# A hybrid decoder step: x turned by VectorE in 32x32 blocks instead of TensorE transposes, with w_in read in the matching row order

## The chip, the cores and the metric

The kernel runs on one core of one Trainium2 chip. The metric is the device time of one execution in microseconds; a kernel's time is the median of its runs. A profile is one execution of its own, recorded by the hardware profiler. In it PE is TensorE's matmul, PEld its weight load, DVE is VectorE, ACT is ScalarE, POOL is GpSimd, and SP is the engine that issues most DMAs.

## The reference

One layer of a hybrid decoder over 256 prompt tokens and 8 x 4 sample tokens, 288 in all, with D = 2048. Cut to what matters here:

```python
def _rmsnorm(x, g):                       # x: (tokens, 2048)
    y = x * lax.rsqrt(jnp.mean(x * x, axis=-1, keepdims=True) + EPS)
    return y * g

xn = _rmsnorm(x, norm_mix)
u = xn @ w_in                             # w_in: (2048, 15408), cut into ten pieces: z, xBC, dt, q, k, v, r, g, gates
...                                       # SSD branch, GLA branch, merged by gates, projected by w_mix_out
h = x + merged                            # the residual
...                                       # cross-attention into 256 memory tokens, then a ConvFFN

mn = _rmsnorm(mem_prompt, norm_mem)       # 256 memory tokens
p_mem_k, p_mem_v = mn @ w_ck, mn @ w_cv   # (256, 2048) each, outputs
```

Everything is float32.

## The kernel before

**Matmuls.** A float32 product is made of three: every operand is split into a high part rounded to fp32r and the low rest, and hi x hi, hi x lo and lo x hi are summed in PSUM. For weights `wsplit` does this: ACT casts `raw` into `whi` (line 103) and DVE subtracts to give `wlo` (line 105). `raw` has three buffers (`RB = 3`) and `whi` and `wlo` five each (`WB = 5`). The loads of `raw` are issued by SP in one queue: a load waits until the buffer three loads back has been split, and what stands behind it in the queue waits too.

**Layout.** The activations stand transposed: channels on the partitions, tokens along the free axis, in 16 k-tiles of 128 channels. `X(k)` gives the high and low part of k-tile k of the normalized x. In the kernel before, channel 128k + p is on partition p of k-tile k, and `proj` reads its weights in the same order ("(k p) n -> p k n").

**The first stages.** `mem_proj` makes one 512-column piece of the memory keys or values: 16 k-tiles of six 128x512 matmuls (lines 315, 316, 319), their weights loaded two k-tiles (512 KB) at a time. The first one, of `w_ck`, is written out by hand and takes the memory rows `mt` in with it, by TensorE transposes. Then `weave` runs two of them beside `x_norm` (the stage of x_norm, 32 k-tiles), and two more beside `x_prep` (the stage of x_prep, 32 k-tiles). `weave(main, bg, n_main, n_bg)` advances the background generator in proportion to the main one.

- `x_norm` loads x in nine pieces (`x_load`, on SP): the 32 sample rows into `xs` and quarters of the 256 prompt rows into `xp`, tokens on the partitions. ACT squares and sums them (line 391) in twelve pieces into `sp4`; `ss` becomes 1/rms for each token. It also makes the per-channel vectors: `vrow` is turned on TensorE and copied to `vcol`. At its end `dg`, a diagonal matrix of `ss`, goes through a matmul with ones (line 431), so that `rtok` holds 1/rms of each token on every partition (a DVE copy, line 432).
- `x_prep` turns x: for each k-tile three 128x128 TensorE transposes into PSUM (line 442), an ACT copy into `xf` (line 445), stored to the DRAM tile `x_d` two k-tiles at a time by SP (line 447), a product with `rtok` on DVE (`xr`, line 449), and the split with the gain `norm_mix` into `X` (lines 184 and 185). Last it turns `srow`, the carried rows of the SSD convolution.

After that come the projection of dt and g (`dt_load`, lines 487 to 495: the first reader of X), more `mem_proj`, and the SSD and GLA branches, whose projections all read `w_in` by `proj`. The residual is read back from `x_d` by `load_x` (line 1334, DMAs of POOL into `hx`) when `w_mix_out` is projected, and added at line 1352.

**What sets the order.** The tile framework orders the instructions of each engine by a simulated timeline (`schedule_with_timeline_sim=True`); the first `mem_proj` is excepted, and a DMA marked `keep_in_program_order` keeps its place. The order inside an engine is then fixed, and engines wait for each other by semaphores.

Of the kernel before, what the change touches and what calls it, by code (L numbers as in the profile page):

```python
# [16 lines left out]
P = 128  # L17
# [25 lines left out]
def hybrid_step(ctx: ExitStack, tc: tile.TileContext, I: dict, O: list):  # L43
# [44 lines left out]
    names = [("norm_mem", 16), ("norm_mix", 16), ("ssd_norm", 16), ("norm_cross", 16), ("norm_ffn", 16),  # L88
# [6 lines left out]
    def vec(name):  # L95
        o, n = vofs[name]
        return vcol[:, o:o + n]
# [59 lines left out]

    def proj(w, c0, ncol, X, nk, cons, row0=0):
        def load(k0, kn):
            return wload(w[row0 + k0 * P:row0 + (k0 + kn) * P, c0:c0 + ncol].rearrange("(k p) n -> p k n", p=P))  # L160
        return proj_w(load, ncol, X, nk, cons)
# [100 lines left out]
    x_d = dram.tile([P, KT, T], F32, name="x_d")  # L262
# [3 lines left out]
    with pool("p0") as p0:  # L266
# [7 lines left out]
        mt = p0.tile([P, 2, D], F32, tag="rows", name="mt")  # L274
# [81 lines left out]
        xp = p0.tile([P, 2, D], F32, tag="rows", name="xp")  # L356
        xs = p0.tile([P, D], F32, name="xs")
        G.memset(xs, 0.0)
        xts = [xp[:, 0, :], xp[:, 1, :], xs]
# [16 lines left out]
        def x_load(n):  # L376

            if n == 0:
                d = nc.sync.dma_start(out=xs[0:NS], in_=I["x_sample"].rearrange("b l d -> (b l) d"))
            else:  # L380
                i, cs = (n - 1) // 4, slice((n - 1) % 4 * 512, (n - 1) % 4 * 512 + 512)
                d = nc.sync.dma_start(out=xp[:, i, cs], in_=I["x_prompt"][0, i * P:(i + 1) * P, cs])
            tc.keep_in_program_order(d)

        def x_norm():
            sp4 = p0.tile([P, 3, 4], F32, name="sp4")
            ss = p0.tile([P, 3], F32, name="ss")

            def square(i, q):
                junk = p0.tile([P, 512], F32, name="junk")  # L390
                S.activation(junk, xts[i][:, q * 512:(q + 1) * 512], ACT.Square, accum_out=sp4[:, i, q:q + 1])

            for step in range(23):
                if step % 2 and step < 18:
                    x_load(step // 2)
                if step == 3:

                    V.tensor_reduce(mrs, mss, AX.X, ALU.add)
                    S.activation(mrs, mrs, ACT.Ln, scale=1.0 / D, bias=epsc[:, 0:1])
                    S.activation(mrs, mrs, ACT.Exp, scale=-0.5)  # L400
                if step == 6:
                    held.pop()()
                if step > 6 and step % 2 == 0 and step < 15:
                    square(2, step // 2 - 4)
                if step > 6 and step % 2:
                    square((step - 7) // 8, (step - 7) // 2 % 4)
                yield
            V.tensor_reduce(ss, sp4, AX.X, ALU.add)
            S.activation(ss, ss, ACT.Ln, scale=1.0 / D, bias=epsc[:, 0:1])
            S.activation(ss, ss, ACT.Exp, scale=-0.5)  # L410
# [15 lines left out]
            dg = p0.tile([P, 3, P], F32, name="dg")  # L426
            for i in range(3):
                V.tensor_scalar(dg[:, i, :], ident, ss[:, i:i + 1], None, ALU.mult)
            yield
            a = mm_tile()  # L430
            MM(a[:, 0:T], ones, dg.rearrange("p c t -> p (c t)")[:, 0:T], start=True, stop=True)
            V.tensor_copy(rtok, a[:, 0:T])
# [3 lines left out]
        def x_prep():  # L436

            gx = vec("norm_mix")
            for k in range(KT):
                a = mm_tile()  # L440
                for i, xt in enumerate(xts):
                    TR(a[:, i * P:(i + 1) * P], xt[:, k * P:(k + 1) * P], ident)
                if k % 2 == 0:
                    xf = p0.tile([P, 2, T], F32, tag="xf", bufs=3, name="xf")
                S.copy(xf[:, k % 2, :], a[:, 0:T])
                if k % 2:
                    nc.sync.dma_start(out=x_d[:, k - 1:k + 1, :], in_=xf)
                xr = p0.tile([P, T], F32, tag="xr", bufs=3, name="xr")
                V.tensor_tensor(xr, a[:, 0:T], rtok, ALU.mult)
                split_from(*X(k), xr, gx[:, k:k + 1])  # L450
                yield
            for q in range(2):
                a = mm_tile()
                for i in range(3):
                    TR(a[:, i * 96:(i + 1) * 96], srow[:, 3 * q + i, :], ident[0:96, 0:96])
                V.tensor_copy(scst[:, q * 12:(q + 1) * 12, 0:3 * NB], a[:, 0:288].rearrange("p (t c) -> p t c", c=3 * NB))
                yield
# [16 lines left out]
        weave(chain(mem_proj(I["w_cv"], 0, o_pmv), mem_proj(I["w_ck"], 1, o_pmk)), x_norm(), 2 * KT, 28)  # L474
# [11 lines left out]
        def dt_load(k0, kn):  # L486
            raw = wp.tile([P, kn, 112], F32, tag="raw", bufs=RB, name="raw")
            for o, c0, n in ((0, O_DT, 32), (32, O_G, 16)):
                nc.sync.dma_start(out=raw[:, :, o:o + n],
                                  in_=I["w_in"][k0 * P:(k0 + kn) * P, c0:c0 + n].rearrange("(k p) n -> p k n", p=P))  # L490
# [841 lines left out]
    def load_x(j2):  # L1332
        m = pc.tile([P, 2, T], F32, tag="hx", bufs=3, name="hx")
        G.dma_start(out=m, in_=x_d[:, 2 * j2:2 * j2 + 2, :])
# [496 lines left out]
```

## Time and profile before

| | |
|---|---|
| median of 3 runs | 2519.35 us (2517.22 to 2526.04) |
| profiled execution | 2522.44 us |
| its span, first to last instruction | 2520.7 us |
| PE busy | 2502.4 us (99%) |
| DVE, ACT, POOL busy | 1753.1, 1346.9, 392.8 us |
| DMA | 521.95 MB, mean 207 GB/s |
| stage of x_norm | about 33 to 76.5 us |
| stage of x_prep | 76.5 to 127.15 us |

The profiled execution is a run of its own, 3.1 us over the median. Busy is the time in which an engine had at least one instruction under way; matmuls overlap, so a matmul's duration is longer than the distance to the next one. A row of a group gives line, engine, operation, output<-inputs, shapes and count, then busy us and mean ns, then the engine's idle time before them and what ended it.

### The profile page before, as it was taken

How to read it: one execution, taken by the hardware profiler on the slowest of the kernel's cores; microseconds unless marked ns; L12 is line 12 of the kernel's file. 1: busy time of each engine (PE TensorE's matmuls, PEld its weight loads, DVE VectorE, ACT ScalarE, POOL GpSimd, SP SyncE). 2: the span in 40 equal slices, each digit the busy share in tenths (PEclk: the TensorE clock that was granted, in tenths of full speed). 3: DMA queues.
4: the chain of work that ended last, by engine and by line, in shares of the span. 5: the costliest groups of instructions: out<-in, count | busy, mean ns of one | idle time of the engine just before them, and what ended most of it. 6: DMA issues, size and time to landing. Idle time of an engine off the chain costs nothing.

```text
span 2520.7 us, 50431 instructions
## 1 busy us (share of the span) xinstructions
PE 2502.4 (99%) x18914; PEld 2411.9 (96%) x18914; DVE 1753.1 (70%) x3752; ACT 1346.9 (53%) x2736; POOL 392.8 (16%) x729
## 2 busy tenths in 40 slices
PE   9999999999999999999999999999999999999998
PEld 8889999998999999999999989999999999999998
DVE  6656777796867666666666677567777677676765
ACT  7655647655463655454445544555555455454545
POOL 3002133342300010000001122402111001020010
PEclk9999999999999999999999999999999999999999
DMA  8776587767868675867778599655555555555553
GB/s 268 221 218 196 171 251 210 228 196 210 245 188 275 183 251 175 248 207 263 202 224 267 180 327 323 213 159 178 170 171 173 170 168 171 170 175 169 168 171 129
DMA packets 442021, 521.95 MB, mean 207 GB/s; under 512 B 26876, under 2 KB 390236, under 8 KB 441712
## 3 DMA queue, kind: packets, MB, share of 16 engines
q1 hardware_dynamic: 407728, 422.34, 54.3%
q0 software_dynamic: 34016, 96.38, 12.0%
q8 instruction: 148, 2.42, 0.4%
q14 instruction: 97, 0.79, 0.1%
q10 hardware_dynamic: 32, 0.01, 0.0%
HBM read 473.13 MB, written 45.48 MB: 206 GB/s over the span
## 4 chain that ended last, share of the span: by engine, by line
PE 95%; DMA 2%; DVE 1%; ACT 1%; issue 0%; POOL 0%; DVEq 0%; ACTq 0%; POOLq 0%
PE acc L148 27%; PE acc L147 27%; PE acc L151 26%; PE acc L315 2%; PE acc L316 2%; PE acc L319 2%; PE la L1541 1%; PE mm L1159 1%; PE la L1150 1%; DMA sqr<-in_state_ssd_dram 1%; PE la L1483 1%; PE mm L1123 1%; DMA sin<-in_state_ssd_dram 1%; DMA raw<-in_w_gla_out_dram 0%; POOL sqr L731 0%
## 5 line engine op out<-in xcount | busy, mean ns | idle before, releaser
L103 ACT CAST whi<-raw 128x512 fp32r<-128x512 f32 x1464 | 897.3, 618 | 1011.9 <-PE acc L148 783.6
L105 DVE TENSOR_TENSOR wlo<-raw,whi 128x512 fp32r<-128x512 f32 x1464 | 997.2, 687 | 607.9 <-ACT whi L103 590.5
L147 PE MATMUL acc<-xn,whi 128*128 128x288 f32 (+1 forms) x1936 | 550.2, 299 | 0.0
L148 PE MATMUL acc<-xn,whi 128*128 128x288 f32 (+1 forms) x1936 | 542.0, 296 | 0.0
L151 PE MATMUL acc<-xn,wlo 128*128 128x288 f32 (+1 forms) x1936 | 414.3, 295 | 0.0
L148 PE MATMUL acc<-hf,whi 128*128 128x288 f32 x1408 | 393.2, 295 | 0.0
L147 PE MATMUL acc<-hf,whi 128*128 128x288 f32 x1408 | 389.0, 292 | 0.0
L147 PEld LDWEIGHTS acc<-xn,whi 128*128 128x128 f32 (+1 forms) x1936 | 364.4, 188 | 9.9 <-issue 7.5
L148 PEld LDWEIGHTS acc<-xn,whi 128*128 128x128 f32 (+1 forms) x1936 | 364.5, 188 | 6.6 <-issue 4.6
L151 PEld LDWEIGHTS acc<-xn,wlo 128*128 128x128 f32 (+1 forms) x1936 | 310.5, 188 | 1.6 <-issue 1.3
L151 PE MATMUL acc<-hf,wlo 128*128 128x288 f32 x1408 | 294.5, 290 | 0.0
L148 PEld LDWEIGHTS acc<-hf,whi 128*128 128x128 f32 x1408 | 264.5, 188 | 0.1
L147 PEld LDWEIGHTS acc<-hf,whi 128*128 128x128 f32 x1408 | 264.0, 188 | 0.1
L151 PEld LDWEIGHTS acc<-hf,wlo 128*128 128x128 f32 x1408 | 226.3, 188 | 0.0
L148 PE MATMUL acc<-pr,whi 128*128 128x288 f32 x704 | 196.6, 295 | 0.0
L147 PE MATMUL acc<-pr,whi 128*128 128x288 f32 x704 | 195.0, 293 | 0.0
L151 PE MATMUL acc<-pr,wlo 128*128 128x288 f32 x704 | 147.4, 290 | 0.0
L147 PE MATMUL acc<-un,whi 128*128 128x288 f32 x512 | 145.3, 300 | 1.2 <-DVE mb L961 0.8
L148 PE MATMUL acc<-un,whi 128*128 128x288 f32 x512 | 143.0, 295 | 0.0
L1655 POOL COPY fsp<-fst 128x16 f32<-128x16 f32 x88 | 37.1, 424 | 656.5 <-DVE av L1667 422.0
L148 PEld LDWEIGHTS acc<-pr,whi 128*128 128x128 f32 x704 | 132.3, 188 | 0.0
L147 PEld LDWEIGHTS acc<-pr,whi 128*128 128x128 f32 x704 | 132.0, 188 | 0.0
(516 smaller groups left out, 4283.4 us busy)
## 6 DMA issues: line engine op xcount, KB each, us to landing
raw<-in_w_in_dram SPq DMA_DIRECT2D x240, 512.0 KB
raw<-in_w_up_dram SPq DMA_DIRECT2D x176, 512.0 KB
raw<-in_w_down_dram SPq DMA_DIRECT2D x88, 512.0 KB
raw<-in_w_cv_dram SPq DMA_DIRECT2D x32, 512.0 KB
raw<-in_w_ssd_out_dram SPq DMA_DIRECT2D x32, 512.0 KB
sin<-in_state_gla_dram POOLq DMA_DIRECT2D x32, 512.0 KB, 5.6
out_dram<-sin SPq DMA_DIRECT2D x32, 512.0 KB
raw<-in_w_gla_out_dram SPq DMA_DIRECT2D x32, 512.0 KB
```

What stands on the lines that cost most here:

```text
L103: S.copy(hi, raw)
L105: V.tensor_tensor(lo, raw, hi, ALU.subtract)
L147: MM(a, hi[:, k, cs], xh, start=(k0 + s0 + k == 0), stop=False)
L148: MM(a, hi[:, k, cs], xl, start=False, stop=False)
L151: MM(a, lo[:, k, cs], xh, start=False, stop=(k0 + s0 + k == nk - 1))
L315: MM(accs[m], mn_hi[:, kk, ms_], hi[:, 0, :], start=(kk == 0), stop=False)
L316: MM(accs[m], mn_lo[:, kk, ms_], hi[:, 0, :], start=False, stop=False)
L319: MM(accs[m], mn_hi[:, kk, ms_], lo[:, 0, :], start=False, stop=(kk == KT - 1))
L1123: MM(a, kt[:, i, k * P:(k + 1) * P], vt[i], start=True, stop=True)
L1150: MM(osa[NS * j:NS * j + NS, :], qdm[:, k, b, :], sins[b][:, k, :], start=False, stop=(q == 1 and k == 0))
L1159: MM(a, kb[:, k * P:(k + 1) * P], vst, start=True, stop=True)
L1655: G.tensor_copy(sp[:, :, 0:2], st.rearrange("p (b k) -> p b k", k=2))
```

## The change

x is loaded as nine blocks of 32 tokens into `xrow`: the 2048 channels of a token are cut into four quarters, which lie on the partitions 32i + t. One DVE transpose of 32x32 blocks for each block, reading every 16th element, gives `xT`, in which channel 16p + k stands on partition p of k-tile k. The gain comes in that order by a DMA (`gmix`), and `w_in` is read in that order by `rows_of`, so that the sum over channels is the same. The squares are taken of the same nine blocks; `fold4` times their sums goes through the matmul with ones, which sums the four quarters, and ACT makes 1/rms of the result by Ln and Exp over 128x288. The 48 TensorE transposes and the `xf` copies are gone; `x_d` is now (2048, 288) in channel order, stored from `xT` in program order and read back by k-tiles of 128 channels. The tile of `mt` grows to nine pieces and shares its place with `xrow`.

In the built program the order on every engine is the same from the projection of dt and g on. Before it, the first DVE transpose stands behind the third-next `wlo` after the memory's sum of squares, the others behind every second or third `wlo`; two of the x loads stand one weight load earlier on SP; and the stores of `x_d` begin behind the first weight load of the stage of x_prep.

```diff
@@ -85,7 +85,7 @@
 
     vcol = const.tile([P, 116], F32, name="vcol")
     scw = const.tile([P, 96], F32, name="scw")
-    names = [("norm_mem", 16), ("norm_mix", 16), ("ssd_norm", 16), ("norm_cross", 16), ("norm_ffn", 16),
+    names = [("norm_mem", 16), ("ssd_norm", 16), ("norm_cross", 16), ("norm_ffn", 16),
              ("b_gla_gate", 8), ("gla_norm", 4), ("ssd_conv_b", 24)]
     vofs = {}
     dcol = const.tile([P, KT], F32, name="dcol")
@@ -155,9 +155,15 @@
                     flush()
                 yield
 
+    def rows_of(w, row0, k0, kn, c0, ncol):
+
+        if w is I["w_in"]:
+            return w.rearrange("(p k) n -> p k n", k=KT)[:, k0:k0 + kn, c0:c0 + ncol]
+        return w[row0 + k0 * P:row0 + (k0 + kn) * P, c0:c0 + ncol].rearrange("(k p) n -> p k n", p=P)
+
     def proj(w, c0, ncol, X, nk, cons, row0=0):
         def load(k0, kn):
-            return wload(w[row0 + k0 * P:row0 + (k0 + kn) * P, c0:c0 + ncol].rearrange("(k p) n -> p k n", p=P))
+            return wload(rows_of(w, row0, k0, kn, c0, ncol))
         return proj_w(load, ncol, X, nk, cons)
 
     def run(*gens):
@@ -259,7 +265,7 @@
     ma_d = dram.tile([P, KT, T], F32, name="ma_d")
     mg_d = dram.tile([P, KT, T], F32, name="mg_d")
     ga_d = dram.tile([P, KT // 2, T], F32, name="ga_d")
-    x_d = dram.tile([P, KT, T], F32, name="x_d")
+    x_d = dram.tile([D, T], F32, name="x_d")
     h_d = dram.tile([P, KT, T], F32, name="h_d")
 
     X = halves(bigr, "xn")
@@ -271,7 +277,7 @@
         S.dma_start(out=mrow, in_=I["norm_mem"].rearrange("(t p) -> t p", p=P))
         S.preload_act_table_set(LNEXP)
         S.copy(epsc[:, 2:3], epsc[:, 0:1])
-        mt = p0.tile([P, 2, D], F32, tag="rows", name="mt")
+        mt = p0.tile([P, 9, 512], F32, tag="rows", name="mt")[:, 0:8].rearrange("p (i q) d -> p i (q d)", i=2)
 
         def mem_load(k0):
             cs = slice(k0 * P, (k0 + 2) * P)
@@ -353,10 +359,10 @@
             run(mem_proj(I["w_ck"], 0, o_pmk, prep_mem, held))
 
 
-        xp = p0.tile([P, 2, D], F32, tag="rows", name="xp")
-        xs = p0.tile([P, D], F32, name="xs")
-        G.memset(xs, 0.0)
-        xts = [xp[:, 0, :], xp[:, 1, :], xs]
+        xrow = p0.tile([P, 9, 512], F32, tag="rows", name="xrow")
+        xT = p0.tile([P, KT, T], F32, name="xT")
+        gmix = p0.tile([P, KT], F32, name="gmix")
+        G.dma_start(out=gmix, in_=I["norm_mix"].rearrange("(p k) -> p k", k=KT))
         G.dma_start(out=dtb, in_=I["ssd_dt_bias"].unsqueeze(1))
         G.dma_start(out=alog, in_=I["ssd_A_log"].unsqueeze(1))
         r = 0
@@ -375,22 +381,19 @@
 
         def x_load(n):
 
-            if n == 0:
-                d = nc.sync.dma_start(out=xs[0:NS], in_=I["x_sample"].rearrange("b l d -> (b l) d"))
-            else:
-                i, cs = (n - 1) // 4, slice((n - 1) % 4 * 512, (n - 1) % 4 * 512 + 512)
-                d = nc.sync.dma_start(out=xp[:, i, cs], in_=I["x_prompt"][0, i * P:(i + 1) * P, cs])
-            tc.keep_in_program_order(d)
+            b = n - 1 if n else 8
+            src = I["x_prompt"][0, 32 * b:32 * b + 32] if n else I["x_sample"].rearrange("b l d -> (b l) d")
+            tc.keep_in_program_order(nc.sync.dma_start(out=xrow[:, b, :], in_=src.rearrange("t (i d) -> i t d", i=4)))
 
         def x_norm():
-            sp4 = p0.tile([P, 3, 4], F32, name="sp4")
-            ss = p0.tile([P, 3], F32, name="ss")
-
-            def square(i, q):
+            ss = p0.tile([P, 9], F32, name="ss")
+
+            def square(b):
                 junk = p0.tile([P, 512], F32, name="junk")
-                S.activation(junk, xts[i][:, q * 512:(q + 1) * 512], ACT.Square, accum_out=sp4[:, i, q:q + 1])
-
-            for step in range(23):
+                S.activation(junk, xrow[:, b, :], ACT.Square, accum_out=ss[:, b:b + 1])
+                V.transpose(xT[:, :, 32 * b:32 * b + 32], xrow[:, b, :].rearrange("p (x j) -> p j x", j=KT))
+
+            for step in range(27):
                 if step % 2 and step < 18:
                     x_load(step // 2)
                 if step == 3:
@@ -400,14 +403,11 @@
                     S.activation(mrs, mrs, ACT.Exp, scale=-0.5)
                 if step == 6:
                     held.pop()()
-                if step > 6 and step % 2 == 0 and step < 15:
-                    square(2, step // 2 - 4)
-                if step > 6 and step % 2:
-                    square((step - 7) // 8, (step - 7) // 2 % 4)
+                if step == 9:
+                    square(8)
+                if step > 10 and step % 2:
+                    square((step - 11) // 2)
                 yield
-            V.tensor_reduce(ss, sp4, AX.X, ALU.add)
-            S.activation(ss, ss, ACT.Ln, scale=1.0 / D, bias=epsc[:, 0:1])
-            S.activation(ss, ss, ACT.Exp, scale=-0.5)
             yield
             a = mm_tile()
             TR(a[:, 0:r], vrow[0:r, :], ident[0:r, 0:r])
@@ -423,31 +423,25 @@
                               drow[64 * e:64 * e + 64, :].rearrange("p (t e) -> p e t", e=2)[:, e, :])
             yield
 
-            dg = p0.tile([P, 3, P], F32, name="dg")
-            for i in range(3):
-                V.tensor_scalar(dg[:, i, :], ident, ss[:, i:i + 1], None, ALU.mult)
+            dg = p0.tile([P, 9, NS], F32, name="dg")
+            V.tensor_tensor(dg, fold4.unsqueeze(1).to_broadcast([P, 9, NS]), ss.unsqueeze(2).to_broadcast([P, 9, NS]), ALU.mult)
             yield
             a = mm_tile()
-            MM(a[:, 0:T], ones, dg.rearrange("p c t -> p (c t)")[:, 0:T], start=True, stop=True)
-            V.tensor_copy(rtok, a[:, 0:T])
+            MM(a[:, 0:T], ones, dg.rearrange("p c t -> p (c t)"), start=True, stop=True)
+            S.activation(rtok, a[:, 0:T], ACT.Ln, scale=1.0 / D, bias=epsc[:, 0:1])
+            S.activation(rtok, rtok, ACT.Exp, scale=-0.5)
 
         rtok = p0.tile([P, T], F32, name="rtok")
 
         def x_prep():
 
-            gx = vec("norm_mix")
             for k in range(KT):
-                a = mm_tile()
-                for i, xt in enumerate(xts):
-                    TR(a[:, i * P:(i + 1) * P], xt[:, k * P:(k + 1) * P], ident)
                 if k % 2 == 0:
-                    xf = p0.tile([P, 2, T], F32, tag="xf", bufs=3, name="xf")
-                S.copy(xf[:, k % 2, :], a[:, 0:T])
-                if k % 2:
-                    nc.sync.dma_start(out=x_d[:, k - 1:k + 1, :], in_=xf)
+                    tc.keep_in_program_order(nc.sync.dma_start(
+                        out=x_d.rearrange("(p k) t -> p k t", k=KT)[:, k:k + 2, :], in_=xT[:, k:k + 2, :]))
                 xr = p0.tile([P, T], F32, tag="xr", bufs=3, name="xr")
-                V.tensor_tensor(xr, a[:, 0:T], rtok, ALU.mult)
-                split_from(*X(k), xr, gx[:, k:k + 1])
+                V.tensor_tensor(xr, xT[:, k, :], rtok, ALU.mult)
+                split_from(*X(k), xr, gmix[:, k:k + 1])
                 yield
             for q in range(2):
                 a = mm_tile()
@@ -471,7 +465,7 @@
         G.affine_select(gm_f, causal, pattern=[[-64, 2], [0, 64]], compare_op=ALU.is_ge, fill=0.0, base=0,
                         channel_multiplier=1)
         V.tensor_copy(gmask, gm_f)
-        weave(chain(mem_proj(I["w_cv"], 0, o_pmv), mem_proj(I["w_ck"], 1, o_pmk)), x_norm(), 2 * KT, 28)
+        weave(chain(mem_proj(I["w_cv"], 0, o_pmv), mem_proj(I["w_ck"], 1, o_pmk)), x_norm(), 2 * KT, 31)
         weave(chain(mem_proj(I["w_cv"], 1, o_pmv), mem_proj(I["w_ck"], 2, o_pmk)), x_prep(), 2 * KT - 2, 18)
 
 
@@ -487,7 +481,7 @@
             raw = wp.tile([P, kn, 112], F32, tag="raw", bufs=RB, name="raw")
             for o, c0, n in ((0, O_DT, 32), (32, O_G, 16)):
                 nc.sync.dma_start(out=raw[:, :, o:o + n],
-                                  in_=I["w_in"][k0 * P:(k0 + kn) * P, c0:c0 + n].rearrange("(k p) n -> p k n", p=P))
+                                  in_=rows_of(I["w_in"], 0, k0, kn, c0, n))
             for k in range(kn):
                 G.tensor_copy(raw[:, k, 48:112].rearrange("p (r n) -> p r n", n=16),
                               raw[:, k, 32:48].unsqueeze(1).to_broadcast([P, 4, 16]))
@@ -1331,7 +1325,7 @@
 
     def load_x(j2):
         m = pc.tile([P, 2, T], F32, tag="hx", bufs=3, name="hx")
-        G.dma_start(out=m, in_=x_d[:, 2 * j2:2 * j2 + 2, :])
+        G.dma_start(out=m, in_=x_d[256 * j2:256 * j2 + 256].rearrange("(t p) n -> p t n", p=P))
         hx.append(m)
 
     for j2 in range(3):
```

## Prediction

> **What bounds the kernel now.** I read the page first: the busy times and the chain that ended last.
>
> ```profile
> span 2520.7 us, 50431 instructions
> PE 2502.4 (99%) x18914; PEld 2411.9 (96%) x18914; DVE 1753.1 (70%) x3752; ACT 1346.9 (53%) x2736; POOL 392.8 (16%) x729
> PE 95%; DMA 2%; DVE 1%; ACT 1%; issue 0%; POOL 0%; DVEq 0%; ACTq 0%; POOLq 0%
> ```
>
> TensorE works all the time, and 95% of the chain is its matmuls. A change pays if it takes time from TensorE's own stream, and costs if it makes TensorE wait. So the next view is the busy time by stretches. The memory projections around the change use 128x512 matmuls, six to a k-tile. Reading the timeline of TensorE, k-tiles 1 to 31 of the stage of x_norm (counted from 0) fill 34.33 to 76.50 us, and the 32 of the stage of x_prep fill 76.50 to 127.15 us.
>
> ```profile
> core 0: us, PE busy (x) PEld busy (x) DVE busy (x) ACT busy (x) POOL busy (x), PEclk, DMA share, GB/s
> 34.33:76.50 42.17, 42.17 (x187) 34.91 (x186) 21.29 (x36) 28.58 (x64) 1.51 (x2) 1.00 0.85 283
> 76.50:127.15 50.65, 50.65 (x249) 41.42 (x248) 36.20 (x69) 34.37 (x71) 5.03 (x16) 1.00 0.70 211
> ```
>
> In both TensorE is busy for the whole stretch, at a granted clock of 1.00: it is the limit. The first gives the price of a k-tile with nothing between, 42.17 / 31 = 1.360 us. The second stage takes 50.65 us where 32 bare k-tiles would take 43.53. What lies between is 7.12 us, and these are its groups:
>
> ```profile
> L442 PE MATMUL mm<-ident,xp 128*128 128x128 f32 x32 | 6.1, 272 | 0.0
> L442 PE MATMUL mm<-ident,xs 128*128 128x128 f32 x16 | 4.4, 273 | 0.0
> L455 PE MATMUL mm<-ident,srow 96*128 96x96 f32 x6 | 0.8, 245 | 0.0
> L431 PE MATMUL mm<-dg,ones 128*128 128x288 f32 x2 | 0.6, 405 | 0.0
> ```
>
> **Part 1: 48 transposes leave TensorE.** The 272 ns are not their price, since matmuls overlap. The price is what they push the next start by:
>
> ```profile
> 81.93 0.40 PE L315 MATMUL acc<-whi,mn_hi 128*128 128x512 f32 x1
> 82.17 0.39 PE L316 MATMUL acc<-whi,mn_lo 128*128 128x512 f32 x1
> ...
> 82.85 0.38 PE L442 MATMUL mm<-ident,xp 128*128 128x128 f32 x2
> 83.07 0.27 PE L442 MATMUL mm<-ident,xs 128*128 128x128 f32 x1
> 83.10 0.48 PE L315 MATMUL acc<-whi,mn_hi 128*128 128x512 f32 x1
> 83.41 0.39 PE L316 MATMUL acc<-whi,mn_lo 128*128 128x512 f32 x1
> ```
>
> From the first transpose of a k-tile (82.85) to the second matmul behind it (83.41) are 0.56 us; two matmuls without transposes stand 0.24 apart (81.93, 82.17). So three transposes cost about 0.33 us, and 16 triples 5.3 us: the lower end. The upper end is the 7.12 us less what stays. The row-scale matmul L431 stays (by its overlap about 0.5 us). The six srow transposes stay, two triples, at the price of the others at most 0.33 us each. They leave 7.12 - 0.5 - 0.6 = 6.0 us, which counts also that matmuls behind a transpose start about 5 ns further apart. I take 6.0, because it is a difference of whole stages. The row-scale matmul and the transposes of the vectors (116 columns, then 100) stay alike within hundredths.
>
> **Part 2: the turns and squares in the stage before.** DVE gains nine 128x512 transposes, ACT loses three of twelve squares.
>
> ```profile
> L882 DVE STREAM_TRANSPOSE st<-sqr 128x512 f32<-128x512 f32 x32 | 21.9, 697 | 0.0
> L1678 DVE STREAM_TRANSPOSE fcs<-cin 128x256 f32<-128x256 f32 x10 | 4.4, 436 | 0.0
> L549 DVE COPY dtbd<-tokc 32x8 f32<-32x8 f32 x4 | 0.7, 167 | 0.1
> L391 ACT ACTIVATE junk<-xp 128x512 f32<-128x512 f32 x8 | 5.0, 630 | 0.2
> L105 DVE TENSOR_TENSOR wlo<-raw,whi 128x512 fp32r<-128x512 f32 x32 | 21.0, 690 | 19.6 <-ACT whi L103 18.5 <-PE acc L319 1.1
> L103 ACT CAST whi<-raw 128x512 fp32r<-128x512 f32 x33 | 19.0, 617 | 13.1 <-DMA raw<-in_w_cv_dram 4.4 <-PE acc L319 4.0 <-DMA raw<-in_w_ck_dram 3.7
> 60.88 1.40 DVE L105 TENSOR_TENSOR wlo<-raw,whi 128x512 fp32r<-128x512 f32 x2 [0.92 <-ACT whi L103]
> 62.44 0.61 PE L319 MATMUL acc<-wlo,mn_hi 128*128 128x512 f32 x2
> ```
>
> The new turns read every 16th element (64 bytes apart), which no transpose of this trace does. Lower bound: 0.70 us (L882, elements side by side). Upper bound: L882 and L1678 give (697 - 436) / 256 = 1.0 ns an element and a fixed 175 ns; the copy L549 reads 8 elements 16 bytes apart in 167 ns, no more than that fixed part, so I allow a second nanosecond an element, 175 + 512 x 2.0 = 1.2 us. Nearest is L882, the same operation and size. In the changed kernel's order a turn stands behind every two or three wlo. Two k-tiles of TensorE last 2.72 us and two wlo 1.38, so DVE has 1.34 us free for each turn: 0.70 and 1.2 both fit. A turn can only cost where TensorE is close behind DVE. The closest place is k-tile 21: its wlo starts at 60.88, ends near 61.6, and is used at 62.44, 0.9 us later. Behind a turn on DVE's queue stand the next wlo, TensorE behind them, and the release of a raw buffer, so the next weight load. In the order, the turns are done by k-tile 19, and the last square stands before the cast of k-tile 20, where it stood between those of 20 and 21. I take 0, and keep 0 to +2 us. The turn waits for its own x load, which SP issues right behind a weight load whose k-tiles come next on DVE anyway. SP has the last two x loads one weight load earlier, 0.25 MB, 0.9 us at the stage's 283 GB/s, for weights that now come later; TensorE's 0.9 us just cover it. The x_sample load, now into the rows buffer, waits for the last read of mem, with the next weight load behind it on SP.
>
> **Part 3: the second stage.**
>
> ```profile
> L445 ACT COPY xf<-mm 128x288 f32<-128x288 f32 x16 | 6.3, 393 | 1.0 <-PE mm L442 0.2
> L449 DVE TENSOR_TENSOR xr<-mm,rtok 128x288 f32<-128x288 f32 x16 | 7.2, 451 | 0.0
> L184 ACT ACTIVATE xn<-xr,vcol 128x288 fp32r<-128x288 f32 x16 | 8.5, 533 | 0.4 <-DVE xr L449 0.2
> 127.15 0.29 PE L147 MATMUL acc<-xn,whi 128*112 128x288 f32 x1
> ```
>
> ACT loses sixteen xf copies (6.3 us) and gains a Ln and an Exp of 128x288, priced by L184 at 0.53 each. With the cast between them, rtok comes some 1.7 us after its matmul instead of 0.45. Behind it wait all xr and xn, but xn is first read at 127.15, and in the new order the last xn stands nine wlo ahead of that stage: cost 0. That order packs the 32 xr and xn and two srow copies between some 18 wlo: 34 x 0.45 (L449) + 18 x 0.69 (L105) = 27.7 us of DVE against 18 x 1.36 = 24.5 us of TensorE. DVE falls 3.2 us back there, out of at most 5 x 1.36 = 6.8 us that the five wlo buffers let it be ahead: 0 again, but the thinnest of the zeros. The eight stores of x_d stand on SP earlier, the first behind the stage's first weight load; it needs the last turn, done by then, so nothing queues behind a wait. Their bytes are the same. The stage's DMA share becomes 0.70 x 50.65 / 44.65 = 0.79; the stage before ran at 0.85 without a wait of TensorE.
>
> **Part 4: x back, and w_in by 16 rows a partition.**
>
> ```profile
> L1352 DVE TENSOR_TENSOR hx<-acc,hx x16: 448/451/458, 1325.4 to 1410.6; 128x288 f32<-128x288 f32 x16
> DMA to landing us min/median/max: 2.9/4.5/9.9
> 250.00:350.00 100.00, 100.00 (x785) 98.85 (x784) 74.35 (x150) 55.93 (x122) 30.76 (x57) 1.00 0.73 216
> q1 hardware_dynamic: 18128, 16.55, 56.3%
> raw<-in_w_in_dram SPq DMA_DIRECT2D x29, 512.0 KB
> ...
> q1 hardware_dynamic: 7295, 6.99, 59.5%
> ...
> q1 hardware_dynamic: 150487, 149.45, 53.3%
> ```
>
> The loads of x_d read pieces of 1152 bytes instead of 2304. Two uses of hx take 85.2 / 8 = 10.7 us and a load is issued two such turns ahead, 21 us; landing took 9.9 us at most, so twice that still fits: 0. A w_in load has as many packets of 1 KB as before; only the distance between partitions grows from 61,632 to 986,112 bytes. The last two rows are 500 to 540 us (mostly w_in) and 1600 to 2500 us (mostly w_up and w_down, rows 45,056 and 8,192 bytes apart): 59.5% x 16 x 40 / 7295 = 52 ns a packet, 53.3% x 16 x 900 / 150487 = 51 ns. Distances from 8 to 62 KB make no difference, and I price the longer one at 0.
>
> **The sum.** TensorE -6.0 us; everything else beside it at 0. The profiled run took 2522.44 us (span 2520.7) and becomes 2516.4; it lies 3.1 us above the median of the three runs (2517.22 to 2526.04). From the median: 2519.35 - 6.0 = **2513.4 us**. That is 0.24%, just inside the 0.3% (7.6 us) that a measurement of this kernel can tell from no change.
>
> **Rivals.**
>
> A, larger gain: the one long wait of TensorE shifts away too.
>
> ```profile
> PE mm L894 <- ACT cst L603: 3.4, 1, 3.4
> 570.00:580.00 10.00, 8.33 (x51) 8.34 (x52) 5.04 (x13) 2.67 (x6) 2.72 (x4) 0.83 0.99 283
> ```
>
> It stands at 568 us, and the clock behind it falls to 0.83 of ten microseconds: 3.4 + 1.7 = 5.1 us. DMA share is 0.99 there, so landing order decides. Against: from the dt projection on, the order on every engine is unchanged, so all moves together. Gone, it gives 2508.3.
>
> B, slower: the strided reads make the turns slow. If a turn takes t, DVE falls back by 8 x (t - 1.34) us over the nine; beyond the 0.9 us of lead TensorE waits. So it starts at 1.45 us, has eaten the 6.0 at 2.2 us, and is slower by 0.3% at 3.2 us. At a fifth of L882's speed (3.45 us): 16.9 - 0.9 - 6.0 = +10, 2529 us. For it: no row reads at 64 bytes. Against: L549 at 16 bytes. [...]
>
> C, slower: the longer distance makes w_in's packets slow. Its 29 loads are 29 x 512 = 14,848 of 18,128 packets, 0.46 of the DMA share of 0.73. DMA becomes the limit there when a packet takes 1.6 times as long; at twice, the share is 1.19, and the 240 loads, 828 us at this pace, cost 0.19 x 828 = 157 us: 2670. Against: 51 and 52 ns at the distances so far. [...]
>
> D, refunded: the time comes back as waits for weights, since the stage of x_norm is near its DMA's limit and TensorE only 0.9 us behind DVE, or in the packed part of the second stage. Between nothing and all 6.0 lost: up to 2519.4. For: the casts' waits for raw in L103's row, 4.4 + 3.7 us. Against: TensorE waited nowhere in these stages, and ACT has less to do in both.
>
> **How the numbers follow.** Forecast 0.66, A 0.08, B 0.08 (0.05 of it slower by over 0.3%), C 0.04, D 0.14. The range reaches to A and to all of D, 2508.3 to 2519.4, and leaves out B, C and the tails. The forecast lies 1.6 us short of the bound, and the runs before lie 8.8 us apart, so over a third of its chance is beyond: 0.25; with A, faster 0.33. Slower is 0.05 + 0.04 = 0.09. The rest, 0.58, is within.
>
> **What would show it.** Right: no transposes of x on TensorE; the second stage about 44.6 us; nine turns of about 0.7 us; no TensorE wait before 140 us; the wait at 568 us now near 562. Wrong: turns above 1.45 us; packets of w_in above 52 ns at 494 to 534 us; a second stage above 46 us; a TensorE wait for wlo in the first two stages.

## The result and the profile after

The changed kernel takes 2526.42 us (median of 12 runs, 2523.73 to 2534.86) where the kernel before takes 2519.31 on the same chip: 1.0030 times as long, interval 1.0017 to 1.0043. The forecast was 2513.4 and the range ended at 2519.4: the change costs some 7 us where 6 were expected back.

The busy times by stretches, changed kernel; the first stretch is k-tiles 1 to 31 of the stage of x_norm, the second the stage of x_prep, both read off TensorE's timeline as before.

```profile
core 0: us, PE busy (x) PEld busy (x) DVE busy (x) ACT busy (x) POOL busy (x), PEclk, DMA share, GB/s
34.33:90.07 55.74, 46.78 (x189) 34.84 (x188) 30.01 (x42) 25.97 (x53) 1.51 (x2) 0.97 0.66 224
90.07:134.88 44.81, 44.81 (x201) 36.84 (x200) 34.03 (x68) 28.84 (x57) 4.16 (x15) 1.00 0.77 232
```

The second stage fell from 50.65 to 44.81 us, as forecast. The first grew from 42.17 to 55.74, 13.6 us, and TensorE is busy in only 46.78 of them. Together X is first read 7.7 us later, and the medians lie 7.1 us apart. (Single traces say less about the whole: from the first use of X to the end they take 2387 us in e12 and 2400 us in e15, the extremes of all kernels below, and the changed kernel's profiled run, 2525.73 us, makes up 4.4 of the 7.7 us there.)

TensorE's longest waits, changed kernel (us in total, times, longest), and the groups that it waits for:

```profile
PE acc L325 <- DVE wlo L105: 9.0, 8, 2.2
PE mm L888 <- ACT cst L597: 1.9, 1, 1.9
```

```profile
L103 ACT CAST whi<-raw 128x512 fp32r<-128x512 f32 x33 | 18.8, 617 | 11.3 <-DMA raw<-in_w_ck_dram 5.3 <-DMA raw<-in_w_cv_dram 3.2 <-DVE wlo L105 2.6
L394 DVE STREAM_TRANSPOSE xT<-xrow 128x512 f32<-128x512 f32 x9 | 9.6, 1064 | 15.7 <-DMA xrow<-in_x_prompt_dram 12.6 <-DMA xrow<-in_x_sample_dram 3.1
```

Eight waits for `wlo`, 9.0 us, stand where none stood. Of the 13.6 us they are 9.0, a lowered clock (last section) is 1.7, and the other 2.9 stand in TensorE's busy time, which these rows do not split. The casts wait for `raw`, 8.5 us here, but that is little more than the 8.1 us before, when TensorE did not wait; new is that VectorE stands 15.7 us in front of turns whose x block has not landed. Two readings were open: the turn, waiting at the head of VectorE's queue, holds up the splits behind it; or all loads are late. The DMA view of 36 to 78 us shows loads: the mean busy share of the sixteen engines in forty slices, and the GB/s of each. The kernel before, then the changed one:

```profile
DMA  9999999999999769769989303979799438868869
GB/s 380 371 271 324 314 417 336 406 402 408 386 295 314 240 162 380 244 248 300 380 242 349 152 12 121 347 191 146 244 380 406 162 31 295 252 199 296 330 179 330
```

```profile
DMA  9824799327722268489327932893495249503997
GB/s 300 312 107 127 236 375 371 137 99 275 291 101 99 101 189 308 168 211 355 113 101 205 343 119 101 205 355 111 142 322 197 101 105 304 219 23 53 363 240 217
```

The changed kernel falls back seven times to 99 to 127 GB/s at a share of 0.2 to 0.4, in stretches of up to 3 us, about what an x load of 256 KB takes at 100 GB/s (2.6 us). Inside one of them the share is 0.26 of sixteen engines, so about four are at work, and by the trace's packet records four packets are under way at once in 90% of it, 86 ns on the mean for 2 KB (columns as in the first table):

```profile
47.60:50.60 3.00, 1.87 (x8) 1.18 (x7) 2.87 (x4) 1.86 (x4) 0.00 (x0) 0.81 0.26 100
```

The x load's source is "t (i d) -> i t d" with `i` = 4 outermost.

That the four steps make the four engines was the author's reading; e7 and e11 below, with 4 and with 2, test it. Which engines they are the trace does not show.

### The profile page after: what moved, and what is told of

It reads as the page before. It is cut to its first block, busy times and chain, and to the rows that moved or that the text cites. A ratio compares the mean times of both kernels' runs of the same rounds, so it can differ in the third digit from the quotient of the medians.

```text
span 2524.0 us, 50293 instructions
## 1 busy us (share of the span) xinstructions
PE 2497.6 (99%) x18866; PEld 2403.5 (95%) x18866; DVE 1755.6 (70%) x3757; ACT 1336.4 (53%) x2714; POOL 391.5 (16%) x728
## 4 chain that ended last, share of the span: by engine, by line
PE 93%; DMA 3%; DVE 2%; issue 1%; ACT 0%; POOL 0%; SPq 0%; DVEq 0%; ACTq 0%; POOLq 0%
PE acc L148 27%; PE acc L147 27%; PE acc L151 26%; PE acc L325 2%; PE acc L321 2%; PE acc L322 2%; DMA xrow<-in_x_prompt_dram 1%; PE mm L1153 1%; PE la L1144 1%; PE la L1477 1%; DVE wlo L105 1%; PE mm L1117 1%; DMA raw<-in_w_ssd_out_dram 0%; PE la L1535 0%; DMA kc<-in_cache_mem_k_dram 0%
```

## The experiments

Times are medians in us; each ratio, with its 95% interval, is to runs of the kernel before on the same chip and need not be the ratio of the medians.

**First theory: the turn in line behind its load.** Four edits of the changed kernel.

```diff
# e1: squares and turns keep the order of the program
-                S.activation(junk, xrow[:, b, :], ...)
+                tc.keep_in_program_order(S.activation(junk, xrow[:, b, :], ...))   # the turn likewise
# e2: the turn reads a constant tile
-                V.transpose(..., xrow[:, b, :].rearrange("p (x j) -> p j x", j=KT))
+                V.transpose(..., xz.rearrange("p (x j) -> p j x", j=KT))
# e3: the squares are of a constant tile
# e4: the turn reads its elements side by side (another order of channels)
+                V.transpose(..., xrow[:, b, :].rearrange("p (j x) -> p j x", j=KT))
```

> The changed kernel with its squares and turns held in the program's order, so that the first turn stands behind twelve wlo instead of three and each other one three to four weight loads behind its own x load; nothing is left out. Theory 'in line behind a load': VectorE's turn waits at the head of its queue for an x block that was asked for behind a weight load not yet needed, and behind it stand the wlo that free the raw buffers that the next weight load needs. Then the waits go: no TensorE wait in the stage of x_norm, the row-scale matmul near 76.5 us (90.1 in the changed kernel, 76.5 before), X first read near 121.3 us (134.9 and 127.2), about 13.6 us less than the changed kernel and 5.8 us less than before: 2513.5. Rival 'slow turns' (1.07 us each instead of 0.70, too much work for VectorE in the stage): the nine turns are as long as ever, the loss stays within 3 us of 13.6: 2524 to 2527. Rival 'w_in rows' (the loss lies in the longer row distance of w_in): unchanged, 2526.

> The changed kernel with the nine turns reading a constant tile instead of the x blocks, so the turn never waits for a load; x is left out of the result, the turn's work, shape and stride stay, the squares still wait for x. In line behind a load, with VectorE as the engine that matters: most of the 13.6 us come back, row-scale matmul at 77 to 80 us (the squares on ScalarE stand one weight load later in their queue than the turns), time 2514 to 2517. Slow turns: no change, row-scale matmul near 90, time 2526. w_in rows: no change, 2526.

> The changed kernel with the nine squares on ScalarE taken of a constant tile instead of the x blocks (the sums of squares are left out of the result); the turns still wait for x. In line behind a load, VectorE's queue being the one that closes the loop: little comes back, row-scale matmul at 87 to 90 us, time 2523 to 2527. If ScalarE's queue closes it (its squares wait 14.6 us in all for x): row-scale matmul at 77 to 80, 2514 to 2517. Slow turns and w_in rows: no change.

> The changed kernel with the turns reading elements side by side instead of every 16th (channels then stand in another order than w_in's, so the result is another; work and waits are the same but for the turn's length). In line behind a load: each turn takes 0.70 instead of 1.07 us, at most 9 x 0.37 = 3.3 us come back, row-scale matmul at 87 to 90, time 2523 to 2526. Slow turns: all of it comes back, row-scale matmul near 77, 2513. w_in rows: no change, 2526.

Measured: e1 2532.94, 1.0049 (1.0031 to 1.0068); e2 2536.35, 1.0069 (1.0042 to 1.0097); e3 2531.76, 1.0041 (1.0025 to 1.0056); e4 2526.03, 1.0019 (1.0003 to 1.0034). The theory fell. In e1 neither turns nor squares wait for a load any more, yet X is first read at 136.15 us for 134.89, and TensorE waits one engine further up. In e2 the turns are done by 12 us. A wait of 4.9 us stands there at 13 us, ahead of the stage, so of the 15.5 us below only 10.6 stand in the stage, and its time is in part the edit's own doing. e3, slower than all that was expected of it, gives no sign that ScalarE's squares close the loop. TensorE's longest group of waits in e1, then in e2:

```profile
PE acc L321 <- ACT whi L103: 10.0, 8, 2.7
```

```profile
PE acc L321 <- ACT whi L103: 15.5, 9, 4.9
```

The turn in line was the last link before TensorE, not what the time hung on: the weights themselves come late. The stretches at 100 GB/s are in all four; GB/s of 36 to 78 us in e1:

```profile
GB/s 275 361 380 310 369 144 103 205 330 107 101 142 335 174 117 150 326 178 101 101 148 314 199 98 137 322 205 99 158 291 230 99 150 320 209 60 74 363 197 386
```

e4 prices the stride of the turn (1066 ns strided, 712 side by side, medians of nine):

```profile
L394 DVE STREAM_TRANSPOSE xT<-xrow x9: 711/712/714, 37.1 to 69.5; 128x512 f32<-128x512 f32 x9
```

The first use of X came 2.2 us earlier (132.72 for 134.89 us); in the time the two intervals overlap.

**Second theory: x loads on four of sixteen engines.** At 25 GB/s (a quarter of 100) an engine takes 82 ns for a 2 KB packet; the median in the trace, changed kernel, 36 to 78 us, is 84. An estimate from that, with x spread evenly over four engines and the weights over sixteen: in the 2.72 us of two k-tiles each of the four has 128 / 4 = 32 packets of x and 256 / 16 = 16 of weights, 48 x 82 = 3.94 us of work. So each x load costs 1.22 us, nine cost 10.9, and the lowered clock (below) 1.7 more: 12.6 of the 13.6 us. The test: cure it in the changed kernel (e5, e6), give it to the kernel before (e7, e11, e12), and try w_in alone (e8).

```diff
# e5: the changed kernel, each x load as four of 32 partitions (e6: and the order of e1)
-            tc.keep_in_program_order(nc.sync.dma_start(out=xrow[:, b, :], in_=src.rearrange("t (i d) -> i t d", i=4)))
+            for i in range(4):
+                tc.keep_in_program_order(nc.sync.dma_start(out=xrow[32 * i:32 * i + 32, b, :],
+                                                   in_=src[:, 512 * i:512 * i + 512]))
# e7: the kernel before, prompt loads 4 outermost (e11: a=2, e12: a=8)
-                d = nc.sync.dma_start(out=xp[:, i, cs], in_=I["x_prompt"][0, i * P:(i + 1) * P, cs])
+                d = nc.sync.dma_start(out=xp[:, i, cs],
+                                      in_=I["x_prompt"][0, i * P:(i + 1) * P, cs].rearrange("(t a) d -> a t d", a=4))
# e8: the kernel before with rows_of alone, for w_in and dt_load
```

> The kernel before, unchanged but that each of its eight 256 KB loads of the prompt names its 128 rows as 4 by 32 with the 4 outermost, so that the rows come in another order (the tokens are permuted); the bytes and the 2 KB packets are the same. No turn, no other order of w_in, no moved step. Theory now (four of sixteen engines): the loads run at about 100 GB/s in stretches of 2.5 to 3 us, TensorE waits for weights in the stage of x_norm, 7 to 14 us in all, its end moves from 76.5 to 84 to 90 us, and the time goes to 2526 to 2533 us. Rivals (turns, their place, w_in): nothing of theirs is in this kernel, so 2519 us.

> The kernel before, with the 128 rows of each prompt load named as 2 by 64 with the 2 outermost (tokens permuted). Each of two engines then has 64 packets of x and 16 of weights for two k-tiles, 80 by 84 ns = 6.7 us for 2.72 us of matmuls: eight loads lose up to 8 x 4.0 = 32 us, the stretches run at about 50 GB/s, and the time is 2546 to 2560 us. If the load's shape mattered in another way than by the count of engines (the order of the rows), it would be near the 2538.8 of the run on four.

> The kernel before, with the 128 rows of each prompt load named as 8 by 16 with the 8 outermost (tokens permuted). Each of eight engines then has 16 packets of x and 16 of weights for two k-tiles, 32 by 84 ns = 2.7 us for 2.72 us of matmuls: just enough, so 2519 to 2525 us, with waits under 2 us. If the order of the rows were what cost the run on four its 18 us, it would be near that.

> The kernel before with one part of the change alone: w_in's rows and dt's columns read in the turned order (rows k + 16 p), so the output is another. Theory now and the prediction: 51 to 52 ns a packet as before, 2519 us within 2. Rival (the rows 16 apart cost the DMA engines more): packets over 52 ns between 494 and 534 us, new waits for weights from 140 us on, and 2522 us or more.

| outermost dimension of the prompt loads, kernel before | us | ratio (interval) | first use of X, us |
|---|---|---|---|
| 128 (unchanged) | 2519 to 2522 | 1 | 127.15 |
| 8 (e12) | 2525.03 | 1.0013 (0.9998 to 1.0029) | 134.24 |
| 4 (e7) | 2538.83 | 1.0072 (1.0055 to 1.0088) | 139.29 |
| 2 (e11) | 2554.82 | 1.0126 (1.0102 to 1.0149) | 161.49 |

One access pattern, the same bytes and packets, no turn and no w_in: 18 us with 4 outermost, 33 with 2. GB/s of 36 to 78 us with 4, then with 2:

```profile
GB/s 82 92 289 361 427 367 345 178 127 349 191 103 117 181 328 146 101 201 332 107 103 199 330 123 101 209 357 115 103 193 371 105 125 345 211 29 226 283 213 98
```

```profile
GB/s 107 259 384 279 70 57 57 250 279 53 51 53 70 273 244 53 51 66 82 287 222 53 51 119 359 107 51 51 51 51 51 137 326 258 300 101 51 51 84 252
```

The stretches stand at 101 to 107 and at 51 to 53 GB/s. With 4 the share in them is 0.2 to 0.3 of sixteen engines by e7's DMA row, much as in the changed kernel; inside one with 2 it is 0.13, about two of them:

```profile
65.50:67.50 2.00, 1.49 (x4) 1.21 (x5) 1.29 (x2) 0.97 (x2) 0.00 (x0) 0.50 0.13 51
```

So x loads on few engines cost time by themselves, without anything else of the change. The order of the rows is other here too, but the changed kernel, whose loads read rows side by side, runs at the same 100 GB/s. The count by packets came out too low each time: it gave 10 us for four (8 x 1.2) where X came 12.1 later, 31 for two where it came 34.3, nothing for eight where it came 7.1 later in the profiled run of e12. That 8 outermost means eight engines was taken for the count, not shown. In e7 the time (18 us) is beyond what was expected and beyond the 12.1 us. In its trace the time from X to the end is 3.9 us longer too: rival A's wait is 5.8 us for 3.4 (2.4 us), and the clock over 560 to 620 us is 0.94 for 0.97 (1.8 us). The rows of w_in cost nothing: e8 2521.14, 1.0003 (0.9990 to 1.0016).

> The kernel after, with each x load issued as four loads of 32 partitions by 512 elements in place of one load whose outermost dimension is 4; the bytes, the 2 KB packets and their places are the same, and SP issues 36 x loads for 9. Theory now (the x load occupies four of the sixteen DMA engines, about 100 GB/s, and the weight load in line behind it on those four rings lands late): no stretch of about 100 GB/s is left in the window 36 to 78 us, its mean comes back from 203 to about 280 GB/s, TensorE's waits for wlo of about 9 us nearly vanish, the stage of x_norm ends near 77 to 79 us for 90 and the first matmul of the second product begins near 122 to 124 us for 134.9; time 2513 to 2516 us. Rival one (the turn, 1.07 us long or at the head of VectorE's line, holds the splits back): the turns are as long and as placed as before, so the time stays at 2525 to 2527. Rival two (w_in's rows in the new order cost the time): no change either, 2525 to 2527.

> The same four loads for one, and the squares and turns kept in the order in which the program writes them. Theory now (four of sixteen engines): the placement is worth little once the loads land in time, 2513 to 2516 us, within 2 us of the run without the fixed order. Rival one (the turn in line behind its load): the fixed order puts a turn behind the splits that go before it in the program, with its load 8 us old by then, and so this kernel is the faster of the two by 3 us or more.

Both 2522.86, 1.0004 (0.9991 to 1.0017, and 0.9993 to 1.0015): 3.6 us below the changed kernel, whose interval begins where theirs end, but not the 2513 to 2516 expected, and the place of the turns makes no difference. TensorE's waits for weights in e5, and its DMA in 36 to 78 us:

```profile
PE acc L325 <- DVE wlo L105: 2.2, 2, 1.6
PE acc L321 <- ACT whi L103: 0.8, 2, 0.6
```

```profile
DMA  9899999999999546989969987393589989637508
GB/s 384 168 256 345 402 283 326 275 228 298 222 230 332 180 141 226 357 166 326 338 193 336 223 275 219 103 326 139 84 304 423 300 293 318 242 76 254 203 0 70
```

The stretches are gone and X is first read at 127.57 us, 7.3 us earlier than in the changed kernel: this is what the four engines cost it, as far as this cure shows. Some 6 us are still missing to the 121.3 that the transposes alone would give (127.15 - 5.84).

**Other queues.** e9 issues the x loads of the changed kernel from GpSimd, e10 from ScalarE (`nc.sync` becomes `nc.gpsimd`, `nc.scalar`).

> The kernel after, with its nine x loads issued by GpSimd's queue in place of SP's; the same access patterns, bytes and packets. Theory now (the x loads of SP's queue run on the same four DMA engines each time, so that those four carry 32 packets of x and 16 of weights in the 2.72 us of two k-tiles, at 84 ns a packet 4.0 us): if GpSimd's queue spreads its loads differently, the stretches at 100 GB/s go, TensorE's waits for wlo fall from 9.0 us to under 3, and the time is 2513 to 2518 us; if it puts them on the same four, 2522 to 2527. [...] Rivals (turn in line, turn length): 2525 to 2527, the turns being as before.

> The kernel after, with its nine x loads issued by ScalarE's queue in place of SP's. If what costs the time is the order in SP's own queue (a weight load stands behind an x load), it goes: 2513 to 2518 us. If it is the load on four engines, which the other queue shares, those four still have 4.0 us of packets for 2.72 us of matmuls: the time stays within 2522 to 2530.

Both missed: 2539.32, 1.0064 (1.0045 to 1.0082), and 2535.66, 1.0049 (1.0033 to 1.0066), slower than the changed kernel. In e9 six of the eight prompt loads stand behind one of two stores of `mp`, which wait for ACT on the same queue, and the x loads landed 11.2 us (median) after their issue. POOL's queue's longest wait, then GB/s of 36 to 78 us:

```profile
POOL out_dram L334 <- ACT mp L333: 34.4, 2, 28.6
```

```profile
GB/s 184 236 207 137 187 178 209 340 262 299 352 226 192 188 181 183 176 236 344 238 174 47 18 66 353 80 74 341 197 224 355 258 293 256 0 316 219 209 193 269
```

The flat stretches at 100 are gone. In the trace's packet records six to eight data packets of GpSimd's queue are mostly under way at once between 37.5 and 39.5 us, with no store of `mp` issued yet, for four on SP's queue in the changed kernel's stretch. So these loads seem to use more engines between them than one of SP's did; which ones, and whether SP's loads take the same four each time, no run shows. VectorE stands 17 us before turns, and behind one of them, which starts after 5.8 us of that, stands a `wlo` for which TensorE waits 2.3 us: there the turn does hold a split up. e10 keeps the stretches at 100. Neither separates queue order from engine count, since the loads also came at other times.

**Where the other 6 us are.** e13 gives the weights as loaded five buffers for three in e6's kernel, in every memory projection, those of the two stages among them; e14 issues its four loads two and two, at one k-tile and the next; e15 is both; e16 is the kernel before with each prompt load in four loads of 32 partitions.

```diff
# e13
-        raw = wp.tile([P, src.shape[1], src.shape[2]], F32, tag="raw", bufs=RB, name="raw")
+        if more is not None and loads[0] % 5 > 2:
+            raw = more.tile([P, src.shape[1], src.shape[2]], F32, tag="raw2", bufs=2, name="raw")
+        else:
+            raw = wp.tile([P, src.shape[1], src.shape[2]], F32, tag="raw", bufs=RB, name="raw")
# e16
+                for g in range(4):
+                    d = nc.sync.dma_start(out=xp[32 * g:32 * g + 32, i, cs],
+                                          in_=I["x_prompt"][0, i * P + 32 * g:i * P + 32 * g + 32, cs])
```

> The kernel with four x loads for one and squares and turns in program order (2522.9 us), with five buffers for the weights as loaded in place of three in the two stages before the first use of X, so that SP can issue up to five weight loads ahead. If what is left of the loss (the first matmul on X at 127.7 us where 121 was to be had) is weights that land late in bursts of DMA, the stage of x_norm ends near 77 us for 82.6 and the time is 2514 to 2518 us. If it is work on VectorE or ScalarE ahead of the splits, the time stays at 2521 to 2524.

> The same kernel of four x loads and fixed order, with three weight buffers, where the four loads of a block are issued two at one k-tile and two at the next in place of four at every other. If the burst of four is what delays the weight load behind it: 2518 to 2521 us; if the mean load of the DMA engines or work on VectorE is: 2521 to 2524.

> Both: five weight buffers, and the x loads two and two. By late weights: 2513 to 2517 us, the best of all. By work on VectorE or ScalarE: 2521 to 2524.

> The kernel before, with each prompt load of 128 partitions split in four loads of 32 partitions by 512 elements; bytes, packets of 2 KB, order of rows and places unchanged. If loads into 32 partitions are slower than into 128, packets in the window 36 to 78 us take about 109 ns on the mean, as with the four loads of the changed kernel, for 98, some waits for whi or wlo appear, and the time is 2522 to 2526 us. If they cost nothing and the rest of the loss is the turns' work: packets at 98 ns, no waits, 2519 to 2521 us.

Measured: e13 2517.47, 0.9992 (0.9983 to 1.0001); e14 2523.36, 1.0008 (0.9998 to 1.0017); e15 2518.28, 0.9990 (0.9980 to 1.0001); e16 2523.73, 1.0016 (1.0007 to 1.0025). The stretch 36 to 78 us of the kernel before, of e16 and of e13 (the columns as above):

```profile
36.00:78.00 42.00, 42.00 (x187) 34.73 (x186) 21.65 (x37) 28.23 (x63) 1.51 (x2) 1.00 0.84 281
```

```profile
36.00:78.00 42.00, 41.49 (x179) 32.86 (x178) 20.25 (x34) 26.84 (x59) 1.51 (x2) 1.00 0.86 265
```

```profile
36.00:78.00 42.00, 40.39 (x173) 31.32 (x172) 27.34 (x40) 23.37 (x50) 1.51 (x2) 1.00 0.89 274
```

GB/s over share is 335 in the kernel before and 308 in both others: loads of 64 KB into 32 partitions kept the DMA engines busy longer for the same bytes (a 2 KB packet's mean in this window goes from 98.0 to 106.7 ns in e16). That alone costs the kernel before 3 us (X at 129.31 us for 127.15). Whether it is the 32 partitions or the four times as many loads, e16 does not separate. Five buffers take 5.4 us off e6 by the medians, 3 by the ratios, and at X 2.8 of the 6.4 us that were missing: part of the rest was weights landing late. Two and two does nothing. Five buffers in the kernel before were not run; TensorE waits nowhere in these stages there. In e13 the stage of x_norm ends at 80.04 us for 76.50 and the stage of x_prep takes 44.81 again:

```profile
80.04:124.85 44.81, 44.81 (x202) 36.83 (x200) 33.15 (x66) 28.41 (x55) 4.80 (x16) 1.00 0.72 230
```

So X comes 2.3 us earlier than in the kernel before, and the median is 3 us lower, with an interval that just touches 1. e13, within what was expected, and e15, 1.3 us above it, are the shortest times run, and neither is told apart from the other or, clear of noise, from the kernel before. What holds the last 3.5 us is left open; candidates are TensorE's waits for `whi` there (1.5 us in two), gaps too short for a row and the slower packets.

## Why the prediction was wrong

**Part 1 was right.** No transposes of x on TensorE; -5.84 us where -6.0 (5.3 to 6.0) was taken, the same in e13.

**Part 2 failed**, in the sentence that priced loads: "SP has the last two x loads one weight load earlier, 0.25 MB, 0.9 us at the stage's 283 GB/s". The bytes are those of before, but 283 GB/s is the rate of this stage in the kernel before, at a share of 0.85 of sixteen engines; the load's new source puts it on four, 2.6 us at 100 GB/s, and that for all nine loads, not for two moved ones. The prediction gave the new shape of the x loads no price at all. The next step leaned on it: "for weights that now come later; TensorE's 0.9 us just cover it". The term was 0 to +2 and measured +13.6. Curing the loads (e5) brought 7.3 us of it back, though the cure's own loads are slower ones (e16: 2.2 us); the turn's stride was 2.2 us (e4), and late weights with three buffers 2.8 us (e13). These were measured in different kernels and need not add up. Of "The turn waits for its own x load, which SP issues right behind a weight load whose k-tiles come next on DVE anyway" the turn did wait, 15.7 us, yet e1 and e2 took that wait away and gained nothing. The turn's length, 1.07 us, lies inside the bounds of 0.70 and 1.2, but the value taken was the lower one. By the prediction's own rule a turn costs nothing below 1.45 us, and still 0.35 us less, nine times, brought X 2.2 us forward in e4. That the late weights had used up VectorE's lead would explain it; no run shows that.

**Part 3 was right**: 44.81 us for 44.65, DMA share 0.77 for 0.79, no wait of TensorE in the stage.

**Part 4 was right.** Between 494 and 534 us, changed kernel (packets, MB, share of sixteen engines):

```profile
q1 hardware_dynamic: 6033, 5.39, 46.2%
```

46.2% x 16 x 40 us / 6033 = 49 ns a packet, under the 52 of the bound, and e8 shows the same in the time. Reading x back appears in none of TensorE's waits.

**The rivals.** A: the wait at 568 us is 1.9 us in the changed kernel, but 4.0 in e1, 1.3 in e13 and 3.4 in e15: it differs between kernels that do the same work there, and a single reading should not have carried a rival. B starts at 1.45 us a turn, and the turns stayed at 1.07. C fell with the packets. D named the place and the kind, waits for weights in the stage of x_norm, and was bounded wrongly: "between nothing and all 6.0 lost" makes a refund of what Part 1 earns, though nothing ties the one to the other. The loss was more than twice the gain, and with D bounded so only 0.09 was left for slower.

## What to carry to other kernels

When a load keeps its bytes but changes its access pattern, look at the outermost dimension of its source before pricing it: with 4 outermost x ran at 100 GB/s (changed kernel, e7), with 2 at 51 (e11), where the same stage reached 400 in the kernel before, and it held back the loads behind it. A GB/s row that returned to the same low value was the signature here, and shaping the same loads of an unchanged kernel (8, 4, 2 outermost) priced it without the rest of the change. The wait tables gave the last link: they named a turn, a split and a cast in turn, and the cause stood only in the DMA rows.

## What the runs showed of the hardware

TensorE's granted clock fell to half for 3.41 us in the changed kernel, 1.5 us after the matmuls had resumed behind the wait of 2.23 us. The timeline of TensorE, and the window of the lowered clock (0.50, third figure from the end):

```profile
43.85 0.73 PE L325 MATMUL acc<-wlo,mn_hi 128*128 128x512 f32 x2 [2.23 <-DVE wlo L105]
44.42 0.40 PE L321 MATMUL acc<-whi,mn_hi 128*128 128x512 f32 x1
44.66 0.39 PE L322 MATMUL acc<-whi,mn_lo 128*128 128x512 f32 x1
...
46.19 0.63 PE L321 MATMUL acc<-whi,mn_hi 128*128 128x512 f32 x1
46.62 0.63 PE L322 MATMUL acc<-whi,mn_lo 128*128 128x512 f32 x1
```

```profile
45.35:48.76 3.41, 2.75 (x7) 1.63 (x5) 1.22 (x2) 0.72 (x2) 0.00 (x0) 0.50 0.59 213
```

Two matmuls stand 0.24 us apart just behind the wait and 0.43 some 2 us later; half of 3.41 us are 1.7 us on top of the wait. The length of a wait alone did not decide it: over 560 to 620 us the clock's mean is 0.97 in the changed kernel, with one wait of 1.9 us there, and 1.00 in e5 and e12, with waits of 2.1 and 2.2 us.

A DVE transpose of 128x512 float32 took 1.07 us reading 64 bytes apart (changed kernel, median 1066 ns) and 0.71 side by side (e4, 712 ns).
